# Embedding projection splits behind the last early sum of the norm, and three modulation steps instead of seven in the first output projection

## Chip, cores and metric

The kernel runs on one core of a Trainium2 chip. The metric is the device time of one execution in microseconds, as the median of several runs. Times inside a run are read from a profile of one execution.

## What is computed

Two transformer-like blocks run one after the other on 256 positions of width 1024, in 32-bit floating point. The first block has two layers. Layer 0 is a retention mixer, layer 1 a latent attention (MLA). Each layer ends alike:

```python
x = x + rms_norm(y, post_norm_g[i])
x = x + (p[i] @ ple_w_proj[i]) * jax.nn.sigmoid(x @ ple_w_gate[i])
```

Here `y` is the output projection of the mixer, `p[i] @ ple_w_proj[i]` the embedding projection (from 256 to 1024) and `x @ ple_w_gate[i]` the gate projection (1024 to 1024). The second block begins with a modulation vector that depends on none of this:

```python
mod = jax.nn.silu(c) @ w_ada[l] + b_ada[l]
```

It has 6 × 1024 entries and is needed only when the second block starts. Convolution, pooling, a merge, layer norms and a feed-forward part follow; the change does not touch them.

## The kernel before

Activations are kept transposed: 128 partitions hold 128 features, 256 columns hold the positions. A 32-bit product is made of three products of the rounded type `fp32r` (function `mm`, lines 237 to 239): high part by high part, high weight by low activation, low weight by high activation. So every weight tile of 128 × 1024 (eight blocks of 128 columns) is first split: ScalarE casts it to the high part (line 178, tile `wh`), VectorE subtracts to get the low part (line 179, tile `wl`). Activations are split in the same way (lines 187 and 188). There are five buffers of `wh`, five of `wl` and six of the raw weights (`raw`), which come in by DMAs that SyncE issues. A sixth `wh` can be written only when TensorE has finished with the first.

Each engine works through its own queue in order. A scheduler fixes these queues when the program is built, from the order in which the code calls the operations, from their dependences and from its own estimate of durations.

*Modulation steps.* The modulation vector is made in 48 steps (`ada_steps`), each a DMA of 128 × 1024 weights and one multiply-and-reduce on VectorE (line 418) with two buffers. They are filled in beside other work. `tick` counts the estimated time of the products, and whenever `mods["rate"]` microseconds have gone by since the last step it issues one, up to 41 in the first block. `mod_rate` sets the pace: 7.61 and later 12.84 in the head pairs of MLA, and an own value in each output projection.

*Output projection and norm.* `out_proj` runs the products of the 16 × 8 weight blocks in two parts: for all eight output blocks the first 12 of 16 row blocks, then, after `drain`, the last four. It sets the pace before the first part and takes it away after it. Between the parts `ple_proj` fetches and splits the embeddings. In the second part, each finished pair of output blocks is handed to a `Sums` object: `feed` squares it on ScalarE (line 332) and adds the squares on VectorE (line 336). Pairs 0 to 2 are fed in this way and so there are two additions, the early sums. `flush` has TensorE add them over the partitions by products with a matrix of ones (line 346). Blocks 6 and 7 are squared (line 362) and summed on TensorE directly by `end`, which makes four sum products of 256 columns in all.

*After the projection.* `post` forms 1/rms on VectorE (lines 384, 372, 375, 378; ScalarE's line 386 lies between the first two). While this runs, TensorE has the embedding projection to do: `prepared`, the inner function of `ple_proj`, makes its 48 products of two weight tiles. Then VectorE scales the projection's blocks (line 695), adds the residual (line 696) and splits the result (line 188), and only then can the gate projection (`half_outer`) start, with its own weight tiles. Line 688 of ScalarE copies the projection's blocks out of the accumulators, line 740 those of the embedding projection.

The two places that hand this to the scheduler, in the code before:

```python
            V.tensor_add(self.tot[0], self.tot[0], sq)
...
            tiles = [seq.next() for _ in range(16)]
...
    ys, prep = out_proj("ret_out", ret_g, 12, 1.8, done, 0)
...
    ys, prep = out_proj("mla_out", mla_g, 12, 2.27, done, 1)
```

Of the kernel before, what the change touches and what calls it, by code (L numbers as in the profile page):

```python
# [82 lines left out]
def tile_kernel(ctx, tc, order, xT, pT, pos, vec, cst, cv, rows, wada, wts, outT):  # L83
    nc = tc.nc
    V, A, T = nc.vector, nc.scalar, nc.tensor
# [11 lines left out]
    def nm(s):  # L97
        uid[0] += 1
        return f"{s}_{uid[0]}"
# [4 lines left out]
    def bank2():  # L104
        return bank().rearrange("p (b t) -> p b t", b=2)
# [20 lines left out]
    def two(nb):  # L126
        return Blk(nb, F32R), Blk(nb, F32R)
# [6 lines left out]
    def t2(dt=F32):  # L134
        return tp.tile([P, 2, S], dt, tag="t2", name=nm("t2"), bufs=6)
# [4 lines left out]
    def small(n):  # L140
        return sp.tile([P, n], F32, tag="small", name=nm("sm"), bufs=8)
# [40 lines left out]
    def nouter(name, ms, kbs, c0=0):  # L182
        return [(name, kb * P, c0 + m * P) for m in ms for kb in kbs]

    def split(hi, lo, src, scale=None):
        if scale is None:
            A.copy(hi, src)  # L187
            V.tensor_sub(lo, src, hi.bitcast(F32))  # L188
        else:
            A.activation(hi, src, AF.Copy, scale=scale)  # L190
            V.scalar_tensor_tensor(lo, src, scale, hi.bitcast(F32), MUL, SUB)
# [18 lines left out]
    def mod_rate(us):  # L210
        mods["rate"], mods["last"] = us, clk[0]
# [13 lines left out]
    def drain():  # L225
        busy[0] = True
        while queue:
            due, fn = queue.pop(0)
            clk[0] = max(clk[0], due)
            fn()  # L230
        busy[0] = False
# [4 lines left out]
    def mm(ps, l, r, first, last):  # L236
        T.matmul(ps, l[0], r[0], start=first, stop=False)  # L237
        T.matmul(ps, l[0], r[1], start=False, stop=False)  # L238
        T.matmul(ps, l[1], r[0], start=False, stop=last)  # L239
        tick(3 * cols(r[0]) / 2400.0)  # L240
# [5 lines left out]
    def rhs(pair, kb):  # L246
        return pair[0][kb], pair[1][kb]
# [76 lines left out]
    class Sums:  # L324
# [5 lines left out]
        def feed(self, x):  # L330
            sq = t2()
            A.activation(sq, x, AF.Square)
            if self.tot is None:
                self.tot = [sq, x]
                return
            V.tensor_add(self.tot[0], self.tot[0], sq)
            if self.both:
                new = self.tot[1] if self.own else t2()
                V.tensor_add(new, self.tot[1], x)
                self.tot[1], self.own = new, True  # L340
# [184 lines left out]
    ret_g = two(16)  # L525
# [97 lines left out]
        after(2.04, lambda h=h: ret_av(h))  # L623


    def out_proj(name, pairs, ka, rate, done, layer):
        ys = proj_banks()
        mod_rate(rate)
        seq = Seq(nouter(name, range(8), range(ka)) + nouter(name, range(8), range(ka, 16)))
        for m in range(8):  # L630
            for kb in range(ka):
                mm(ys.at(m), seq.next(), rhs(pairs, kb), ys.starts(m) and kb == 0, False)
        drain()
        mod_rate(None)
        prep = ple_proj(layer)
        for m in range(8):
            for kb in range(ka, 16):
                mm(ys.at(m), seq.next(), rhs(pairs, kb), False, kb == 15 and ys.ends(m))
            if ys.ends(m):
                done(m, ys)  # L640
        return ys, prep
# [20 lines left out]
    def proj_sums(both, get, key):  # L662

        sums = Sums(both, 0)

        def done(m, ys):
            x = get(m, ys)
            if m < 6:
                sums.feed(x)
                if m == 5:  # L670
                    after({"r": 2.0, "m": 0.96}[key], sums.flush)
            elif m == 6:
                after({"r": 1.28, "m": 1.06}[key], lambda: sums.end(x, False))
            else:
                drain()
                sums.end(x, True)
        return sums, done
# [4 lines left out]
    def post(x, ys, sums, layer, prepared):  # L682

        x1 = Blk(DB)

        def scaled(ks):
            for k in ks:
                A.activation(x1[k], ys.at(k), AF.Copy, scale=pgh[:, layer * 8 + k:layer * 8 + k + 1])
        scaled(range(3))
        nry = rms_neg2(sums.ps[0], D)  # L690
        scaled(range(3, DB))
        prj = prepared()
        x1p = two(DB)
        for k, n in ((0, 1), (1, 1), (2, 2), (4, 2), (6, 1), (7, 1)):
            V.tensor_mul(x1.span(k, n), x1.span(k, n), bc2(nry, n))  # L695
            V.tensor_add(x1.span(k, n), x1.span(k, n), x.span(k, n))
            split(x1p[0].span(k, n), x1p[1].span(k, n), x1.span(k, n))
        x2 = Blk(DB)

        def fin(ps, k, n):  # L700
            sgm = t2()[:, :n, :]
            A.activation(sgm, ps, AF.Sigmoid)
            V.tensor_mul(sgm, sgm, prj.span(k, n))
            V.tensor_add(x2.span(k, n), sgm, x1.span(k, n))

        half_outer(f"ple_gate{layer}", x1p, fin)
        return x2
# [14 lines left out]
                    mm(q[:, b, :], seq.next(), rhs(xpair, kb), kb == 0, kb == nk - 1)  # L722
            fin(q, k, n)

    def ple_proj(layer):
        php = [tp.tile([P, 2, S], F32R, tag="fa", name=nm("php"), bufs=3) for _ in range(2)]
        raw = t2()
        nc.gpsimd.dma_start(out=raw, in_=pT[:, 2 * layer:2 * layer + 2, :])
        split(php[0], php[1], raw)

        def prepared():
            seq = Seq(nouter(f"ple_proj{layer}", range(8), range(2)))
            tiles = [seq.next() for _ in range(16)]
            prj = Blk(DB)
            for i in range(4):
                ps = bank2()
                for b in range(2):
                    for kb in range(2):
                        mm(ps[:, b, :], tiles[(2 * i + b) * 2 + kb], (php[0][:, kb, :], php[1][:, kb, :]), kb == 0, kb == 1)
                A.copy(prj.pair(i), ps)  # L740
            return prj
        return prepared

    sums, done = proj_sums(False, lambda m, ys: ys.piece(m), "r")
    ys, prep = out_proj("ret_out", ret_g, 12, 1.8, done, 0)
    xt = post(xt, ys, sums, 0, prep)


# [54 lines left out]
    seq = Seq([e for kb in range(8) for e in (("mla_kr", kb * P, 0), ("mla_in", kb * P, 768), ("mla_in", kb * P, 896))])  # L803
# [9 lines left out]
    seq = Seq(nouter("mla_in", range(6), range(8)))  # L813
# [25 lines left out]
    mla_g = two(16)  # L839
# [116 lines left out]
        after(3.07, lambda p=p: mla_scores(p))  # L956

    sums, done = proj_sums(False, lambda m, ys: ys.piece(m), "m")
    ys, prep = out_proj("mla_out", mla_g, 12, 2.27, done, 1)
    xt = post(xt, ys, sums, 1, prep)  # L960


# [396 lines left out]
    seq = Seq([e for i in range(NA + 2, FB) for e in nouter("w_up", [i, FB + i], range(8))])  # L1359
# [13 lines left out]
    ka = 17  # L1373
    seq = Seq([("w_down", kb * P, 512 * n) for kb in kbs for n in range(2)], 512)
# [30 lines left out]
    for tb in range(2):  # L1405
# [19 lines left out]
        sq, r = small(1), small(1)  # L1425
# [86 lines left out]
```

## Time and profile before

| what | value |
|---|---|
| median of 3 runs | 838.72 us (838.4 to 840.28) |
| time of the profiled execution | 841.12 us |
| its span, first to last instruction | 839.3 us |
| mean granted clock of TensorE | 0.995 |
| TensorE busy, products / weight loads | 824.9 us (98%) / 787.8 us (94%) |
| VectorE busy | 701.7 us (84%) |
| ScalarE busy | 552.0 us (66%) |
| DMA | 167.49 MB, mean 200 GB/s |

Products of TensorE overlap, so its busy time only shows that something was in flight, not that it ran at its best pace. What it lost is seen better where a product starts late after the one before it. In the profile PE is TensorE, DVE is VectorE, ACT is ScalarE, and L336 is line 336 of the kernel. A row of a timeline gives the start and the duration of an instruction (or of several alike, then x3), its tiles as output<-inputs, and in brackets how long the engine had stood idle before it and what ended that.

### The profile page before, as it was taken

The numbers are of one execution on the slowest core, as the hardware profiler recorded it, in microseconds if no ns is written. First come the engines' busy times: TensorE is split into PE (matmuls) and PEld (weight loads), VectorE is DVE, ScalarE is ACT, GpSimd is POOL, SyncE is SP. The second block draws the span as 40 slices with busy tenths as digits, with TensorE's granted clock in tenths as the row PEclk, the third lists the DMA queues.
The fourth block names the chain that finished last, engine by engine and source line by source line (L and its number), as shares of the span: only waits on it lengthen the run. The fifth ranks groups of instructions, "written<-read, shape, count | busy, mean of one in ns | idle before, by whom it ended". The sixth has DMA issues, their size and how long they took to land.

```text
span 839.3 us, 15764 instructions
## 1 busy us (share of the span) xinstructions
PE 824.9 (98%) x6114; PEld 787.8 (94%) x6114; DVE 701.7 (84%) x1283; ACT 552.0 (66%) x967; POOL 9.9 (1%) x30
## 2 busy tenths in 40 slices
PE   8999999999999999999999999999999999999995
PEld 6989899999999999999999999899998999999885
DVE  6999797898889979699864767899687888889986
ACT  7756465645677676788754867998755576666551
POOL 0000000000000000000000000000000000000001
PEclk9999999999999999999999999999999999999999
DMA  8866567778557748365355365245463455567722
GB/s 324 335 241 222 199 245 247 254 257 308 171 187 242 259 150 279 125 226 190 107 195 176 111 216 175 77 166 196 141 242 114 146 184 194 179 221 252 274 81 76
DMA packets 46779, 167.49 MB, mean 200 GB/s; under 512 B 5360, under 2 KB 5616, under 8 KB 46704
## 3 DMA queue, kind: packets, MB, share of 16 engines
q1 hardware_dynamic: 46080, 164.38, 56.1%
q0 software_dynamic: 624, 2.10, 0.8%
q8 instruction: 48, 0.79, 0.4%
q14 instruction: 27, 0.22, 0.1%
HBM read 165.41 MB, written 1.05 MB: 198 GB/s over the span
## 4 chain that ended last, share of the span: by engine, by line
PE 87%; DVE 7%; DMA 3%; ACT 1%; issue 1%; SPq 0%; DVEq 0%
PE ps L238 25%; PE ps L239 24%; PE ps L237 24%; PE ps L243 11%; DMA adach<-in_wada 3%; DVE wl L179 2%; PE ps L346 1%; PE ps L368 1%; DVE adach L418 1%; DMA half<-in_xT 1%; PE ps L925 1%; DVE half L695 0%; ACT wh L178 0%; DVE half L614 0%; DVE t L378 0%
## 5 line engine op out<-in xcount | busy, mean ns | idle before, releaser
L237 PE MATMUL ps<-half,wh 128*128 128x256 f32 x1504 | 424.9, 283 | 0.0
L238 PE MATMUL ps<-half,wh 128*128 128x256 f32 x1504 | 423.4, 282 | 0.6 <-DVE half L188 0.5
L239 PE MATMUL ps<-half,wl 128*128 128x256 f32 x1504 | 421.7, 281 | 0.9 <-DVE wl L179 0.9
L178 ACT CAST wh<-raw 128x1024 fp32r<-128x1024 f32 x233 | 243.2, 1049 | 156.4 <-PE ps L238 91.4
L179 DVE TENSOR_TENSOR wl<-raw,wh 128x1024 fp32r<-128x1024 f32 x233 | 282.3, 1219 | 57.5 <-ACT wh L178 55.3
L238 PEld LDWEIGHTS ps<-half,wh 128*128 128x128 f32 x1504 | 283.2, 188 | 1.9 <-DVE half L188 0.9
L239 PEld LDWEIGHTS ps<-half,wl 128*128 128x128 f32 x1504 | 283.5, 189 | 1.1 <-DVE wl L179 1.1
L237 PEld LDWEIGHTS ps<-half,wh 128*128 128x128 f32 x1504 | 282.7, 188 | 1.2 <-ACT half L187 0.5
L243 PE MATMUL ps<-half,raw 128*128 128x256 f32 (+2 forms) x384 | 84.9, 380 | 0.0
L243 PEld LDWEIGHTS ps<-half,raw 128*128 128x128 f32 x384 | 72.5, 190 | 10.0
L237 PE MATMUL ps<-wh,half 128*128 128x512 f32 (+1 forms) x202 | 73.1, 362 | 1.1 <-ACT wh L178 1.1
L238 PE MATMUL ps<-wl,half 128*128 128x512 f32 (+1 forms) x202 | 71.5, 354 | 0.5 <-DVE wl L179 0.5
L239 PE MATMUL ps<-wh,half 128*128 128x512 f32 (+1 forms) x202 | 71.7, 355 | 0.0
L418 DVE CUSTOM_DVE_ANT_0 adach<-adach,siluc 128x1024 f32<-128x1024 f32 x48 | 58.4, 1218 | 14.2 <-DMA adach<-in_wada 14.2
L237 PEld LDWEIGHTS ps<-wh,half 128*128 128x128 f32 x202 | 38.2, 190 | 7.0 <-ACT wh L178 1.9
L1092 ACT ACTIVATE t<-apad,vec 128x256 f32<-128x256 f32 x106 | 44.2, 498 | 0.5 <-DVE half L1093 0.5
L238 PEld LDWEIGHTS ps<-wl,half 128*128 128x128 f32 x202 | 38.4, 190 | 6.1 <-DVE wl L179 1.0
L239 PEld LDWEIGHTS ps<-wh,half 128*128 128x128 f32 x202 | 38.3, 189 | 5.6
L1093 DVE TENSOR_TENSOR half<-half,t 128x512 f32<-128x512 f32 x53 | 36.4, 687 | 3.7 <-ACT t L1092 1.8
L187 ACT CAST half<-t 128x256 fp32r<-128x256 f32 (+1 forms) x47 | 20.3, 453 | 13.9 <-DVE t L1352 10.9
L188 DVE TENSOR_TENSOR half<-t,half 128x256 fp32r<-128x256 f32 (+1 forms) x47 | 21.6, 481 | 4.0 <-ACT half L187 3.1
L1347 ACT ACTIVATE t<-ps,vec 128x256 f32<-128x256 f32 x38 | 20.9, 556 | 2.0 <-PE ps L239 1.2
(291 smaller groups left out, 905.7 us busy)
## 6 DMA issues: line engine op xcount, KB each, us to landing
raw<-in_wts SPq DMA_DIRECT2D x257, 512.0 KB, 4.2
adach<-in_wada SPq DMA_DIRECT2D x48, 512.0 KB, 5.3
half<-in_xT SPq DMA_DIRECT2D x4, 256.0 KB, 6.0
half<-in_rows POOLq DMA_DIRECT2D x2, 512.0 KB, 4.5
out<-t SPq DMA_DIRECT2D x4, 256.0 KB, 2.0
cst<-in_cst SPq DMA_DIRECT2D x1, 928.0 KB, 11.0
raw<-in_wts SPq DMA_DIRECT2D x2, 256.0 KB, 4.5
siluc<-in_cv SPq DMA_DIRECT2D x1, 512.0 KB, 7.8
```

The source lines that it names most:

```text
L178: A.copy(hi, raw)
L179: V.tensor_sub(lo, raw, hi.bitcast(F32))
L187: A.copy(hi, src)
L188: V.tensor_sub(lo, src, hi.bitcast(F32))
L237: T.matmul(ps, l[0], r[0], start=first, stop=False)
L238: T.matmul(ps, l[0], r[1], start=False, stop=False)
L239: T.matmul(ps, l[1], r[0], start=False, stop=last)
L243: T.matmul(ps, w, r, start=first, stop=last)
L418: V.tensor_tensor_reduce(ch, ch, sc, 1.0, 0.0, MUL, ADD, mod[:, n:n + 1])
L1092: A.activation(t[:, b, :], apad[:, i0 + b, k:k + S], AF.Copy, scale=w[b])
L1093: V.tensor_add(acc.pair(i0 // 2), acc.pair(i0 // 2), t)
L1347: A.activation(t[:, b, :], ps[:, b, :], AF.Identity, bias=col("b_dw_f_2", m), scale=w[2])
```

## The change

It has two parts. First, the 16 calls that take the two weight tiles of the embedding projection out of the sequence now stand in a block that orders their VectorE instructions behind the addition that `feed` made last. So the two splits (line 179) of these tiles come behind the second early sum in VectorE's queue, in both layers. The casts on ScalarE and the DMAs are not ordered by it. `feed` keeps the instruction for this, and `sums` is passed on through `out_proj` and `ple_proj`. Second, the pace of modulation steps in the first output projection goes from 1.8 to 2.27 us, the value that the second one has already. The number of steps up to the end of the first block stays 41.

```diff
--- before.py
+++ after.py
@@ -333,7 +333,7 @@
             if self.tot is None:
                 self.tot = [sq, x]
                 return
-            V.tensor_add(self.tot[0], self.tot[0], sq)
+            self.added = V.tensor_add(self.tot[0], self.tot[0], sq).ins
             if self.both:
                 new = self.tot[1] if self.own else t2()
                 V.tensor_add(new, self.tot[1], x)
@@ -623,7 +623,7 @@
         after(2.04, lambda h=h: ret_av(h))
 
 
-    def out_proj(name, pairs, ka, rate, done, layer):
+    def out_proj(name, pairs, ka, rate, done, layer, sums):
         ys = proj_banks()
         mod_rate(rate)
         seq = Seq(nouter(name, range(8), range(ka)) + nouter(name, range(8), range(ka, 16)))
@@ -632,7 +632,7 @@
                 mm(ys.at(m), seq.next(), rhs(pairs, kb), ys.starts(m) and kb == 0, False)
         drain()
         mod_rate(None)
-        prep = ple_proj(layer)
+        prep = ple_proj(layer, sums)
         for m in range(8):
             for kb in range(ka, 16):
                 mm(ys.at(m), seq.next(), rhs(pairs, kb), False, kb == 15 and ys.ends(m))
@@ -722,7 +722,7 @@
                     mm(q[:, b, :], seq.next(), rhs(xpair, kb), kb == 0, kb == nk - 1)
             fin(q, k, n)
 
-    def ple_proj(layer):
+    def ple_proj(layer, sums):
         php = [tp.tile([P, 2, S], F32R, tag="fa", name=nm("php"), bufs=3) for _ in range(2)]
         raw = t2()
         nc.gpsimd.dma_start(out=raw, in_=pT[:, 2 * layer:2 * layer + 2, :])
@@ -730,7 +730,8 @@
 
         def prepared():
             seq = Seq(nouter(f"ple_proj{layer}", range(8), range(2)))
-            tiles = [seq.next() for _ in range(16)]
+            with tc.issue_after(sums.added):
+                tiles = [seq.next() for _ in range(16)]
             prj = Blk(DB)
             for i in range(4):
                 ps = bank2()
@@ -742,7 +743,7 @@
         return prepared
 
     sums, done = proj_sums(False, lambda m, ys: ys.piece(m), "r")
-    ys, prep = out_proj("ret_out", ret_g, 12, 1.8, done, 0)
+    ys, prep = out_proj("ret_out", ret_g, 12, 2.27, done, 0, sums)
     xt = post(xt, ys, sums, 0, prep)
 
 
@@ -956,7 +957,7 @@
         after(3.07, lambda p=p: mla_scores(p))
 
     sums, done = proj_sums(False, lambda m, ys: ys.piece(m), "m")
-    ys, prep = out_proj("mla_out", mla_g, 12, 2.27, done, 1)
+    ys, prep = out_proj("mla_out", mla_g, 12, 2.27, done, 1, sums)
     xt = post(xt, ys, sums, 1, prep)
```

The scheduler makes new queues from it. In the rows below names ending in numbers are single buffers, and line numbers from 734 on are one higher in the changed kernel.

VectorE, layer 0, from the last output projection weights to 1/rms; before, with the two embedding tiles `wl_2471` and `wl_2477` first, then three gate tiles:

```order
L179 TENSOR_TENSOR wl_2471<-raw_2468,wh_2470 128x1024
L179 TENSOR_TENSOR wl_2477<-raw_2474,wh_2476 128x1024
L179 TENSOR_TENSOR wl_2573<-raw_2570,wh_2572 128x1024
L336 TENSOR_TENSOR t_386_2339<-t_386_2339,t_390_2371 128x512
L179 TENSOR_TENSOR wl_2603<-raw_2600,wh_2602 128x1024
L336 TENSOR_TENSOR t_386_2339<-t_386_2339,t_394_2404 128x512
L179 TENSOR_TENSOR wl_2633<-raw_2630,wh_2632 128x1024
L384 TENSOR_SCALAR t_404_2453<-ps_2434 128x256
L372 TENSOR_TENSOR t_407_2458<-t_405_2455 128x256
L375 TENSOR_TENSOR t_408_2460<-t_404_2453,t_407_2458 128x256
L378 SCALAR_TENSOR_TENSOR t_406_2457<-t_408_2460,t_405_2455 128x256
```

And now, with the embedding tiles `wl_2458` and `wl_2464` behind the two additions, and four gate tiles from `wl_2560` to `wl_2650`:

```order
L336 TENSOR_TENSOR t_382_2326<-t_382_2326,t_386_2358 128x512
L336 TENSOR_TENSOR t_382_2326<-t_382_2326,t_390_2391 128x512
L179 TENSOR_TENSOR wl_2458<-raw_2455,wh_2457 128x1024
L179 TENSOR_TENSOR wl_2464<-raw_2461,wh_2463 128x1024
L179 TENSOR_TENSOR wl_2560<-raw_2557,wh_2559 128x1024
L179 TENSOR_TENSOR wl_2590<-raw_2587,wh_2589 128x1024
L384 TENSOR_SCALAR t_400_2440<-ps_2421 128x256
L179 TENSOR_TENSOR wl_2620<-raw_2617,wh_2619 128x1024
L372 TENSOR_TENSOR t_403_2445<-t_401_2442 128x256
L179 TENSOR_TENSOR wl_2650<-raw_2647,wh_2649 128x1024
L375 TENSOR_TENSOR t_404_2447<-t_400_2440,t_403_2445 128x256
L378 SCALAR_TENSOR_TENSOR t_402_2444<-t_404_2447,t_401_2442 128x256
```

The additions stand together in front. The gate tiles have moved into the chain of 1/rms, and a fourth one, which stood behind the chain, is ahead of line 375. In layer 1 the same happens, one place later: there the gate splits stand ahead of lines 384, 372, 375 and 378, one each, the fourth ahead of line 378.

ScalarE at the same place, before; `wh_2632` is the cast of the third gate tile and `wh_2662` that of the fourth:

```order
L332 ACTIVATE t_394_2404<-ps_1844 128x512
L688 ACTIVATE half_2449<-ps_1844,pgh 128x256
L362 ACTIVATE t_400_2442<-ps_1845 128x256
L688 ACTIVATE half_2449<-ps_1844,pgh 128x256
L688 ACTIVATE half_2449<-ps_1845,pgh 128x256
L178 CAST wh_2632<-raw_2630 128x1024
L322 ACTIVATE sm_2435<-t_386_2339,eps_r 128x1
L362 ACTIVATE t_401_2445<-ps_1846 128x256
L688 ACTIVATE half_2449<-ps_1846,pgh 128x256
L386 ACTIVATE t_405_2455<-ps_2434,eps_r 128x256
L740 COPY half_2480<-ps_2482 128x512
L178 CAST wh_2662<-raw_2660 128x1024
```

And now, with `wh_2619` the third and `wh_2649` the fourth:

```order
L332 ACTIVATE t_390_2391<-ps_1844 128x512
L688 ACTIVATE half_2436<-ps_1844,pgh 128x256
L362 ACTIVATE t_396_2429<-ps_1845 128x256
L688 ACTIVATE half_2436<-ps_1844,pgh 128x256
L322 ACTIVATE sm_2422<-t_382_2326,eps_r 128x1
L688 ACTIVATE half_2436<-ps_1845,pgh 128x256
L178 CAST wh_2619<-raw_2617 128x1024
L362 ACTIVATE t_397_2432<-ps_1846 128x256
L688 ACTIVATE half_2436<-ps_1846,pgh 128x256
L741 COPY half_2467<-ps_2469 128x512
L386 ACTIVATE t_401_2442<-ps_2421,eps_r 128x256
L178 CAST wh_2649<-raw_2647 128x1024
```

The third cast still stands ahead of the square of block 7 (`t_397_2432`), the fourth still behind line 386; line 322 and one copy of line 740 (now 741) have changed places with their neighbours. On TensorE, the two sum products of `flush` have moved three products forward, and the last sum product of layer 0 stands behind eight products of the embedding projection instead of two, that of layer 1 behind two instead of thirteen.

VectorE, layer 0, the first part of the output projection, from the scaling of the last retention head (line 614) on; before:

```order
L614 SCALAR_TENSOR_TENSOR half_1693<-half_1693,t_342_2007 128x512 x2
L418 ISA adach_2132,mod<-adach_2132,siluc 128x1024
L418 ISA mod 128x1
L188 TENSOR_TENSOR half_158<-half_1693,half_154 128x512 x2
L179 TENSOR_TENSOR wl_2203<-raw_2200,wh_2202 128x1024
L418 ISA adach_2159,mod<-adach_2159,siluc 128x1024
L418 ISA mod 128x1
L418 ISA adach_2186,mod<-adach_2186,siluc 128x1024
L418 ISA mod 128x1
L179 TENSOR_TENSOR wl_2240<-raw_2237,wh_2239 128x1024
```

And now:

```order
L614 SCALAR_TENSOR_TENSOR half_1693<-half_1693,t_340_2001 128x512 x2
L179 TENSOR_TENSOR wl_2194<-raw_2191,wh_2193 128x1024
L188 TENSOR_TENSOR half_158<-half_1693,half_154 128x512 x2
L179 TENSOR_TENSOR wl_2227<-raw_2224,wh_2226 128x1024
L179 TENSOR_TENSOR wl_2260<-raw_2257,wh_2259 128x1024
L418 ISA adach_2222,mod<-adach_2222,siluc 128x1024
```

The split of the third weight tile after line 614 (`wl_2240`, now `wl_2227`) has no modulation step between itself and line 614. Up to the embedding splits there are three steps in place of seven. Four have moved to the last head pairs of MLA, among the scaled scores (lines 904 to 914).

## Rows read from the trace of the kernel before

**Rows 1.** Waits of TensorE: engine, tile, line, waited for; total us, times, longest.

```profile
PE ps L239 <- DVE wl L179: 0.9, 1, 0.9
...
PE ps L346 <- DVE t L336: 0.9, 1, 0.9
```

**Rows 2.** Timeline, TensorE, first output projection and norm: start, us, instruction, idle before.

```profile
192.11 0.28 PE L237 MATMUL ps<-half,wh 128*128 128x256 f32 x1
...
192.23 0.28 PE L238 MATMUL ps<-half,wh 128*128 128x256 f32 x1
...
193.43 0.39 PE L239 MATMUL ps<-half,wl 128*128 128x256 f32 x1 [0.92 <-DVE wl L179]
...
211.36 1.53 PE L346 MATMUL ps<-t,ones 128*128 128x256 f32 x6 [0.92 <-DVE t L336]
...
212.54 0.47 PE L237 MATMUL ps<-php,wh 128*128 128x256 f32 x1
...
212.97 0.59 PE L346 MATMUL ps<-t,ones 128*128 128x256 f32 x2
...
219.57 0.39 PE L238 MATMUL ps<-half,wh 128*128 128x256 f32 x1 [0.26 <-DVE half L188]
```

**Rows 3.** Timeline, VectorE, the same stretch.

```profile
191.00 1.23 DVE L418 CUSTOM_DVE_ANT_0 adach<-adach,siluc 128x1024 f32<-128x1024 f32 x1 [1.01 <-DMA adach<-in_wada]
...
205.39 3.49 DVE L179 TENSOR_TENSOR wl<-raw,wh 128x1024 fp32r<-128x1024 f32 x3
...
210.53 0.68 DVE L336 TENSOR_TENSOR t<-t,t 128x512 f32<-128x512 f32 x1
```

**Rows 4.** Timeline, ScalarE, the same stretch.

```profile
208.49 0.59 ACT L332 ACTIVATE t<-ps 128x512 f32<-128x512 f32 x1
...
210.37 1.05 ACT L178 CAST wh<-raw 128x1024 fp32r<-128x1024 f32 x1
...
216.15 1.05 ACT L178 CAST wh<-raw 128x1024 fp32r<-128x1024 f32 x1 [0.78 <-PE ps L238]
```

**Rows 5.** Timeline, TensorE, second norm.

```profile
470.44 0.59 PE L346 MATMUL ps<-t,ones 128*128 128x256 f32 x2
...
475.84 0.39 PE L238 MATMUL ps<-half,wh 128*128 128x256 f32 x1 [0.28 <-DVE half L188]
```

**Rows 6.** Timeline, VectorE, second norm.

```profile
472.50 0.42 DVE L375 TENSOR_TENSOR t<-t,t 128x256 f32<-128x256 f32 x1
...
472.96 0.43 DVE L378 SCALAR_TENSOR_TENSOR t<-t,t 128x256 f32<-128x256 f32 x1
...
475.37 0.75 DVE L188 TENSOR_TENSOR half<-half,half 128x256 fp32r<-128x256 f32 x2
```

**Rows 7.** Timeline, ScalarE, second norm.

```profile
465.44 0.59 ACT L332 ACTIVATE t<-ps 128x512 f32<-128x512 f32 x1
...
472.29 1.05 ACT L178 CAST wh<-raw 128x1024 fp32r<-128x1024 f32 x1 [0.29 <-PE ps L238]
...
476.20 0.58 ACT L740 COPY half<-ps 128x512 f32<-128x512 f32 x1
```

**Rows 8.** Timeline, VectorE, scores of a late head pair.

```profile
400.44 0.17 DVE L909 RECIPROCAL sm<-sm 128x2 f32<-128x2 f32 x1 [0.46 <-ACT sm L907]
...
403.34 0.17 DVE L909 RECIPROCAL sm<-sm 128x2 f32<-128x2 f32 x1 [0.73 <-ACT sm L907]
...
403.54 0.55 DVE L914 TENSOR_SCALAR sm<-sm,sm 128x128 f32<-128x128 f32 x2
```

**Rows 9.** Timeline, TensorE, transposes of the same head pair.

```profile
405.62 0.82 PE L925 MATMUL ps<-ident,sm 128*128 128x128 f32 x6
```

**Rows 10.** Windows: us, busy by engine (instructions), granted clock, DMA share, GB/s.

```profile
5.00:11.00 6.00, 4.38 (x12) 1.73 (x10) 3.54 (x8) 4.29 (x9) 0.00 (x0) 1.00 0.99 352
...
11.00:15.80 4.80, 4.27 (x13) 3.14 (x12) 4.80 (x12) 4.14 (x7) 0.00 (x0) 0.66 1.01 392
...
208.00:220.00 12.00, 10.83 (x82) 10.23 (x81) 10.20 (x19) 9.02 (x19) 0.00 (x0) 1.00 0.61 219
```

## Prediction

> **What bounds the kernel now.** TensorE sets the time. I read the waits of TensorE first, then its timeline, then the timelines of the two engines that feed it. Its products of 256 columns start 0.12 us apart, as the first two show [rows 2], and the waits list has only two entries near 1 us inside the program that this change can touch [rows 1]. Both lie in the first output projection and the norm behind it. At 192.23 a product waits for a split that VectorE could not begin, because a modulation step ahead of it in VectorE's queue waited 1.01 us for its data [rows 2, 3]; TensorE loses 193.43 − 192.23 − 0.12 = 1.08. At 211.36 the first sum product waits 0.92 for the last addition of squares (line 336), which stands behind three splits back to back and one more [rows 2, 3]. In front of the gate projection come the small waits at 219.57 and 475.84 [rows 2, 5]. So perhaps 2.5 us could be won, and the question is what the new queue orders cost.
>
> **The change, part by part.** Times below are on the clock of the profile shown, whose own run took 841.12 us; that is 2.4 above the median of 838.72, so I sum differences and add them to the median. About 1.7 us, 0.2%, is what a measurement of this kernel can tell from no change.
>
> *Pace 2.27 instead of 1.8.* The order shows three modulation steps in VectorE's queue between the last retention head and the embedding splits where there were seven. At 192 the steps ahead of the needed split are gone: it stands right behind the splits of the head, and its cast is long made. That wait goes: **−1.08**. If another stall took its place, this term would be 0. The four steps reappear behind the scores of the last head pairs. There VectorE scales the probabilities until 403.54 + 0.55 = 404.09, and the transposes begin at 405.62: 1.53 in hand, and 0.27 more for the second three [rows 8, 9]. Three steps at 1.14 each (a pitch taken from VectorE's splits of the same size: 3.49 for three, less overlap [rows 3]) are 3.42; VectorE's idle time there takes up 0.46 + 0.73 [rows 8]. That leaves 0.43 late; the splits that move around it could make it nothing. I take **+0.3**, ends 0 and 1.3 (a data wait like the 1.01 at 191.00 on top [rows 3]).
>
> *The splits behind the last early sum, first norm.* The addition now follows the one before it at once. Its square ends on ScalarE at 208.49 + 0.59 = 209.08 [rows 4]; 0.68 for the addition and 0.15 to TensorE (211.36 against 210.53 + 0.68 [rows 2, 3]) give 209.94, and TensorE gets there at about that time: the 0.92 wait is gone. But the new order of TensorE puts three weight products between the sum products, and eight embedding products instead of two ahead of the last one. A sum product takes 0.39 (three in 212.54 − 211.36), and two embedding products with the change of operand type 0.43 [rows 2], so 0.19 for the change. 209.94 + 2 × 0.39 + (0.19 + 3 × 0.12) + 0.39 + (0.19 + 8 × 0.12) = 212.81. The last sum is at **212.8, where it was at 212.97**: little of the gain is left, and ScalarE could not serve it much sooner, since a cast of 1.05 now stands ahead of its last square [rows 4].
>
> Then comes the step that decides. Behind the sum VectorE forms 1/rms in four operations (lines 384, 372, 375, 378), scales, adds the residual and splits; only then can the gate products run. Before, all three gate splits that have a buffer stood ahead of this chain, and the fourth behind it. Now a *fourth* gate split stands ahead of line 375. It needs a cast (line 178), and the cast a weight buffer: there are five, the two embedding tiles and three gate tiles hold them, so the fourth must wait until TensorE has finished the first embedding tile, 24 of the 48 embedding products. The trace shows this wait: the cast at 216.15 was released by TensorE, 3.18 after the last sum product [rows 2, 4]. With six more embedding products ahead of the sum it comes 3.18 − 6 × 0.12 = 2.46 after it: 215.27. Cast 1.05, split 1.14: line 375 starts at 217.46. From there the order is the one that the second norm already has in this trace: 475.37 − 472.50 = 2.87 to the first split, 0.47 more to the product behind it [rows 5, 6]. So 220.80 instead of 219.57: **+1.23**. TensorE's own work would be done at 212.81 + 0.39 + 0.19 + 40 × 0.12 = 218.2, so it stands still for over 2 us.
>
> *Second norm.* The addition moves from behind a split to 465.44 + 0.59 = 466.03 [rows 7]; with 0.68 and 0.15 TensorE can start summing at 466.86. Five products lie between, one sum product, two embedding products: 466.86 + 0.78 + 0.79 + 0.39 + 0.43 = 469.25 for the last sum (470.44 before [rows 5]). Here the fourth split stands even later in the chain, ahead of line 378. Its cast came 472.29 − 470.44 = 1.85 after the last sum, with thirteen embedding products ahead of that; now two, so 1.85 + 11 × 0.12 = 3.17 after it: 472.42 [rows 5, 7]. Plus 1.05 and 1.14: line 378 at 474.61. From it 475.37 − 472.96 = 2.41, and 0.47 [rows 5, 6]: 477.49. ScalarE also has a fifth cast and a copy of 0.58 [rows 7] ahead of the cast of the first block, both waiting for the end of the embedding products, which could add some 0.3. 477.6 against 475.84: **+1.8**.
>
> The bounds: the delay is nothing (each norm as before, less the early sum) or as computed plus a split's 1.14 in each, if the queue waits once more. No arithmetic, no transfer and no semaphore of its own is added; the splits are only ordered on VectorE.
>
> Sum: −1.08 + 0.3 + 1.23 + 1.8 = **+2.3**, and 838.72 + 2.3 = **841.0 us**.
>
> **TensorE's clock.** Rows first: in the stretch before 11 us TensorE was busy 4.38 of 6.00, and in the next 4.80 the granted clock averaged 0.66, a part of it at 1.2 GHz; around the stalls of the first norm, 10.83 busy of 12.00, it stayed at 1.00, 2.4 GHz [rows 10]. The Trainium skill (TensorE: Matmul & The Clock Gate, Part 1) says that idle TensorE falls back to half rate and advises against long gaps between bursts. By it the stalls made here would also slow what follows; the trace agrees at the start of the program, and no row of before shows a stall of over 2 us later on. The sum above goes without it, since the only longer stalls shown left the clock alone; as a rival it is priced below.
>
> **Rivals.**
> 1. *The embedding products cover the chain* (not slower). If the fourth split turned out not to hold lines 375 and 378, each chain would run from the last sum as it does now: 219.57 − 212.97 = 6.60 and 475.84 − 470.44 = 5.40 [rows 2, 5]. The first norm would give 219.41 (−0.16), the second 474.65, bounded by TensorE's own end (469.25 + 0.39 + 0.19 + 46 × 0.12 = 475.35, about −0.3). With −1.08 and +0.3 this is −1.2, 837.5 us; without the term for the last heads, and with the last square served a split's time earlier, −2.3, 836.4. It decides at the point where the fourth cast ends before line 384 has finished. Against it stands the release by TensorE at 216.15 [rows 4]; for it, only that an inferred releaser could be wrong. Chance 0.12.
> 2. *The chain is held, but for less*: the buffer is free sooner, or line 375 is reached later anyway. Half of 1.23 + 1.8 gives +0.7, 839.5. Chance 0.2.
> 3. *The forecast*, 841.0, itself 840.4 to 842.2. Chance 0.45.
> 4. *The clock falls as well.* The mean 0.66 over 4.80 us means about 3.3 us at half rate [rows 10], so 1.6 lost for each fall. One fall gives 842.6, two 844.2. For it: the stalls grow to twice what the trace has shown harmless. Against: weight products run densely on both sides. Chance 0.18.
> 5. *The slower pace does not help*: the reduced steps still wait for data, in another place ahead of a needed split, and the 1.08 stays: 842.1. The first norm's gain is then gone too. The step's own data wait of 1.01 [rows 3] speaks for it, four fewer transfers in that stretch against it. Chance 0.05.
>
> **How the numbers follow.** Slower by more than 1.7 (above 840.4) are case 3, less its lower edge, and cases 4 and 5: 0.63. Within 1.7 (837.0 to 840.4) are case 2, the lower edge of 3 and most of case 1: 0.30. Faster is the far end of case 1: 0.07. The range leaves out that far end and the second clock fall: 838.6 to 843.6.
>
> **What would show it.** Right: TensorE's waits at 192 and 211 gone; two new waits of 1.5 to 2.5 us in front of the gate products, released by line 188 on VectorE or line 187 on ScalarE; on VectorE a split ahead of line 375 (first norm) and line 378 (second) whose idle time is ended by a cast, and that cast released by TensorE. Wrong: if lines 375 and 378 follow line 372 without an idle stretch, the decisive step has failed; if the last sum lands more than 0.5 before 212.8 plus the shift of the stretch, the cost of the first norm is too high; if the granted clock leaves 1.00 behind a norm, case 4 is at work.

## The result and the profile after

The changed kernel takes **845.07 us** (844.0 to 846.06), the kernel before in the same comparison 839.55 (838.4 to 840.5): a ratio of 1.0054, 95% interval 1.0034 to 1.0074, so some 2.9 to 6.2 us more. The forecast was 841.0 in a range of 838.6 to 843.6: right in its direction, too small in its size. The profiled execution has a span of 843.2 against 839.3, of which 0.55 in the other direction comes from the start of the program, where TensorE ran at half rate for a while in the profile before (granted clock 0.66 from 11 to 15.8 us [rows 10]) and not in this one (1.00).

The waits of TensorE after (total us, times, longest):

```profile
PE ps L237 <- ACT half L187: 3.8, 2, 1.9
...
PE ps L239 <- DVE wl L179: 0.8, 1, 0.8
```

The waits of [rows 1] are gone (what is left for line 179 lies at 30 us). In their place stand two of 1.9, one in each norm, in front of the gate products. TensorE's timeline, first norm:

```profile
211.00 0.70 PE L346 MATMUL ps<-t,ones 128*128 128x256 f32 x2
...
216.13 0.28 PE L239 MATMUL ps<-php,wl 128*128 128x256 f32 x1
218.33 0.63 PE L237 MATMUL ps<-half,wh 128*128 128x256 f32 x3 [1.92 <-ACT half L187]
...
221.40 0.41 PE L237 MATMUL ps<-half,wh 128*128 128x256 f32 x1
221.62 0.41 PE L238 MATMUL ps<-half,wh 128*128 128x256 f32 x1
...
222.25 0.28 PE L238 MATMUL ps<-half,wh 128*128 128x256 f32 x1
222.37 0.28 PE L239 MATMUL ps<-half,wl 128*128 128x256 f32 x1
```

The last embedding product starts at 216.13, the first gate product at 218.33. Then something that [rows 2] do not have: gate products start 0.21 apart until 222.04 and 0.12 apart again from 222.25. The windows over the two norms give the clock (columns as in [rows 10]):

```profile
217.00:221.00 4.00, 2.52 (x12) 2.31 (x13) 4.00 (x11) 2.23 (x5) 0.00 (x0) 0.73 0.76 307
221.00:225.00 4.00, 4.00 (x31) 4.00 (x31) 3.06 (x6) 1.73 (x3) 0.00 (x0) 0.85 0.04 5
474.00:478.00 4.00, 2.15 (x18) 1.94 (x16) 3.97 (x9) 3.09 (x6) 0.00 (x0) 1.00 0.97 362
478.00:482.00 4.00, 4.00 (x22) 3.95 (x22) 4.00 (x9) 0.62 (x1) 0.00 (x0) 0.57 0.33 133
```

Behind both waits the granted clock leaves 1.00: for a time TensorE runs at 1.2 GHz, 22 products in 478 to 482 where 36 have room. What made the wait is on VectorE, first norm:

```profile
207.35 0.69 DVE L336 TENSOR_TENSOR t<-t,t 128x512 f32<-128x512 f32 x1 [2.13 <-ACT t L332]
207.96 4.62 DVE L179 TENSOR_TENSOR wl<-raw,wh 128x1024 fp32r<-128x1024 f32 x4
212.51 0.42 DVE L384 TENSOR_SCALAR t<-ps 128x256 f32<-128x256 f32 x1
212.84 1.21 DVE L179 TENSOR_TENSOR wl<-raw,wh 128x1024 fp32r<-128x1024 f32 x1
213.97 0.41 DVE L372 TENSOR_TENSOR t<-t 128x256 f32<-128x256 f32 x1
214.63 1.23 DVE L179 TENSOR_TENSOR wl<-raw,wh 128x1024 fp32r<-128x1024 f32 x1 [0.24 <-ACT wh L178]
215.77 0.42 DVE L375 TENSOR_TENSOR t<-t,t 128x256 f32<-128x256 f32 x1
```

Between the last addition and line 375 stand six splits, 1.14 each, with 0.24 of idle time in all. ScalarE beside it:

```profile
212.96 0.48 ACT L386 ACTIVATE t<-ps,eps_r 128x256 f32<-128x256 f32 x1 [0.16 <-DVE t L384]
213.55 1.05 ACT L178 CAST wh<-raw 128x1024 fp32r<-128x1024 f32 x1
...
216.38 1.04 ACT L178 CAST wh<-raw 128x1024 fp32r<-128x1024 f32 x1 [0.75 <-PE ps L238]
217.33 0.58 ACT L741 COPY half<-ps 128x512 f32<-128x512 f32 x1
217.87 0.74 ACT L187 CAST half<-half 128x256 fp32r<-128x256 f32 x2
```

The cast of the fourth gate split (213.55) follows line 386 with no wait for TensorE. The last product that reads the buffer which this cast needs is in the trace too, and so is the same place in the second norm (VectorE, then ScalarE):

```profile
213.19 0.28 PE L238 MATMUL ps<-php,wh 128*128 128x256 f32 x1
...
473.57 0.42 DVE L375 TENSOR_TENSOR t<-t,t 128x256 f32<-128x256 f32 x1
473.97 1.22 DVE L179 TENSOR_TENSOR wl<-raw,wh 128x1024 fp32r<-128x1024 f32 x1
475.11 0.42 DVE L378 SCALAR_TENSOR_TENSOR t<-t,t 128x256 f32<-128x256 f32 x1
...
476.24 0.75 DVE L696 TENSOR_TENSOR half<-half,half 128x256 f32<-128x256 f32 x2
...
472.88 1.06 ACT L178 CAST wh<-raw 128x1024 fp32r<-128x1024 f32 x1 [0.75 <-PE ps L238]
...
476.65 0.58 ACT L741 COPY half<-ps 128x512 f32<-128x512 f32 x1
477.13 0.71 ACT L187 CAST half<-half 128x256 fp32r<-128x256 f32 x2
```

In the second norm VectorE has no idle time between line 375, the fourth gate split and line 378, though the cast of that split was released by TensorE. And the new x, whose first block VectorE has added by 476.66 (the first of the two at 476.24), is cast only at 477.13, right behind a copy. In the first norm the cast follows within 0.09 us (217.78, 217.87), so ScalarE adds some 0.4 of its own in the second.

### The profile page after: what moved, and what is told of

It reads as the page before. It is cut to its first block, busy times and chain, and to the rows that moved or that the text cites. A ratio compares the mean times of both kernels' runs of the same rounds, so it can differ in the third digit from the quotient of the medians.

```text
span 843.2 us, 15759 instructions
## 1 busy us (share of the span) xinstructions
PE 827.5 (98%) x6114; PEld 790.3 (94%) x6114; DVE 700.6 (83%) x1283; ACT 553.1 (66%) x967; POOL 9.9 (1%) x30
## 4 chain that ended last, share of the span: by engine, by line
PE 89%; DVE 5%; ACT 2%; DMA 2%; issue 1%; SPq 0%; DVEq 0%; ACTq 0%
PE ps L238 25%; PE ps L239 25%; PE ps L237 25%; PE ps L243 11%; DVE wl L179 1%; DMA raw<-in_wts 1%; PE ps L346 1%; PE ps L368 1%; ACT wh L178 1%; DMA half<-in_xT 1%; DMA adach<-in_wada 1%; PE ps L926 1%; DVE adach L418 0%; DVE half L695 0%; PE ps L1176 0%
```

## The experiments

Each ran beside the kernel before on one chip; ratios are to that. The table comes from the traces: how much later than in the trace before a product of the same number in TensorE's order starts, at the end of a stretch less at its beginning (us; stretches on the clock before, added products left out). "Clock" is TensorE's granted clock, the mean over all runs. Each row is one profiled execution: from 235 to 420 us the kernels lose at three places, near 285, 325 and 386 us, which change from profile to profile, so that a difference of some tenths in that column says little.

| kernel | ratio, interval | 185–206 | first norm 206–235 | 235–420 | second norm 462–495 | clock |
|---|---|---|---|---|---|---|
| before | 1 | 0 | 0 | 0 | 0 | 0.997 |
| changed | 1.0054, 1.0034–1.0074 | −1.21 | 2.53 | −0.21 | 2.97 | 0.993 |
| changed, again (e9) | 1.0045, 1.0028–1.0063 | −1.21 | 2.69 | −0.27 | 3.03 | 0.994 |
| e1 pace alone | 0.9975, 0.9958–0.9993 | −1.21 | −0.80 | 0.85 | 0.00 | 0.997 |
| e2 order alone | 1.0037, 1.0015–1.0060 | −0.58 | 1.40 | 0.26 | 3.04 | 0.994 |
| e6 order in first norm | 1.0013, 0.9999–1.0027 | −1.21 | 2.43 | 0.08 | 0.01 | 0.996 |
| e7 order in second norm | 1.0012, 0.9999–1.0026 | −1.21 | −0.79 | 0.73 | 1.51 | 0.995 |
| e4 gate splits behind 1/rms | 1.0011, 0.9992–1.0031 | −1.21 | 2.81 | 0.53 | 0.04 | 0.995 |
| e8 and ScalarE's order | 0.9995, 0.9984–1.0005 | −1.21 | 0.19 | 0.60 | 0.05 | 0.997 |
| e3 waits filled, 8 long | 1.0052, 1.0034–1.0070 | −1.21 | 1.99 | 1.89 | 2.75 | 0.996 |
| e5 waits filled, 4 long | 1.0052, 1.0033–1.0071 | −1.21 | 1.19 | 1.12 | 1.51 | 0.996 |
| e10 waits filled, 14 short | 1.0035, 1.0024–1.0047 | −1.21 | 1.13 | 0.70 | 1.51 | 0.997 |
| e11 pace alone and 14 short | 1.0013, 0.9998–1.0028 | −1.21 | 0.26 | 1.24 | 0.93 | 0.997 |

**e1: the pace alone.**

```diff
-            with tc.issue_after(sums.added):
-                tiles = [seq.next() for _ in range(16)]
+            tiles = [seq.next() for _ in range(16)]
```

> The pace of 2.27 alone, with the splits queued as before. Theory A (the two parts are independent; the slower pace removes the stall of 1.08 at 192 us, the harm sits in the two norms): the stall at 192 is gone, both norms look as before with the 0.92 wait at 211 and no wait over 0.6 in front of the gate products, the four moved steps cost 0 to 0.3, and the time is 838.3 to 838.8 against 839.55 for the kernel before. Theory B (part of the loss is the moved steps in the last head pairs): TensorE stands still for 1 us or more between 390 and 415 us, and the time is 840 or more.

Measured: ratio 0.9975, some 2.1 us gained, where 0.75 to 1.25 were expected; the interval, 0.6 to 3.5 us, holds both. The wait at 192 is gone. The one at 211, which was expected to stay, shrinks from 0.92 to 0.15 us, though the embedding splits still stand ahead of the addition. VectorE, first norm, in this kernel:

```profile
204.63 0.68 DVE L336 TENSOR_TENSOR t<-t,t 128x512 f32<-128x512 f32 x1
206.31 1.23 DVE L179 TENSOR_TENSOR wl<-raw,wh 128x1024 fp32r<-128x1024 f32 x1 [1.00 <-ACT wh L178]
207.45 0.68 DVE L336 TENSOR_TENSOR t<-t,t 128x512 f32<-128x512 f32 x1
...
210.53 0.42 DVE L384 TENSOR_SCALAR t<-ps 128x256 f32<-128x256 f32 x1 [0.17 <-PE ps L346]
```

In [rows 3] three splits ran back to back into the addition: VectorE was behind. The trace before has six modulation steps of 1.14 each between 188 us and the addition, that of e1 three. Both wait for the data of such steps (1.01 and 1.68 before, 2.95 in e1), so it is the number of steps that differs. With three fewer VectorE is early, idles 1.00 before a split and makes the addition at 207.45. Of the two stalls that bounded the kernel the pace removes one and all but 0.15 of the other; hardly anything is left for the second part of the change to win. Most of the 0.85 in the next stretch is a wait of 0.56 at 285 us for a split of the latents, which stands behind a weight split there; between 390 and 415 us TensorE doesn't stand still for the moved steps.

**e2: the order alone.**

```diff
-    ys, prep = out_proj("ret_out", ret_g, 12, 2.27, done, 0, sums)
+    ys, prep = out_proj("ret_out", ret_g, 12, 1.8, done, 0, sums)
```

> The splits behind the last early sum alone, with the pace of 1.8. Theory A: both norms show the wait of about 2 us in front of the gate products and about 18 products at half rate behind each; the stall at 192 is back. Time of the changed kernel plus 1.1: 845.7 to 846.7. Theory B (the moved steps carry a part): 844 or less. If the steps that now stand near the norm delay its splits, the waits in front of the gate products would be longer than 2.0.

Measured: 1.0037, 845.26 us where its baseline was 841.13. By this difference of 4.1 the time is under what theory A gave (6.1 to 7.1 over 839.55) and within theory B; by the trace theory A holds, since both waits are there, but half of the stall at 192 stays away (−0.58). Nor do the two parts add up: 0.9975 and 1.0037 give 1.0012 together, 3.5 us under the changed kernel. In the traces 1.4 of these are counted twice (the stall at 211, 0.80 in e1's first norm, and the 0.58 at 192, which each part removes by itself); the rest is not explained and lies within the intervals. TensorE in the first norm:

```profile
216.65 0.28 PE L239 MATMUL ps<-php,wl 128*128 128x256 f32 x1
218.85 0.62 PE L237 MATMUL ps<-half,wh 128*128 128x256 f32 x3 [1.92 <-ACT half L187]
219.63 0.39 PE L238 MATMUL ps<-half,wh 128*128 128x256 f32 x1 [0.16 <-DVE half L188]
219.85 0.28 PE L239 MATMUL ps<-half,wl 128*128 128x256 f32 x1
219.97 0.28 PE L237 MATMUL ps<-half,wh 128*128 128x256 f32 x1
```

The same wait of 1.92, but products 0.12 apart right behind it: here the clock stayed at 2.4 GHz, and the first norm costs 1.40, not 2.53. In the second norm of the same execution it fell (0.57 in 478 to 482), and that costs 3.04.

**e6, e7: the order in one norm only** (with the pace of 2.27; e7 has `layer == 1`).

```diff
-            with tc.issue_after(sums.added):
+            if layer == 0:
+                with tc.issue_after(sums.added):
+                    tiles = [seq.next() for _ in range(16)]
+            else:
                 tiles = [seq.next() for _ in range(16)]
```

> Pace 2.27, and the splits behind the last early sum in the first norm only. By the traces of the changed kernel and of the pace alone the first norm costs 3.6 us (wait 2.0 and half-rate products 1.7), the second nothing: pace alone (ratio 0.9975, -2.1 us) + 3.6 = +1.5 us, ratio 1.0018, where the first wait lets the clock fall; +0.1 us, ratio 1.000, where it does not. Rival: the two norms are not independent (the first one's delay shifts the transfers of what follows), and the sum of both single costs misses the changed kernel by over 1.5 us.

> Pace 2.27, and the splits behind the last early sum in the second norm only. By the traces the second norm costs 3.0 us (wait 2.0, half-rate products 1.7, less the small wait of 0.4 that is there anyway and 0.3 of the sum): -2.1 + 3.0 = +0.9 us, ratio 1.001. Rival: as for the first norm; a ratio under 0.999 or over 1.0035 would show that the norms hang together.

Measured: 1.0013 and 1.0012. Each norm adds 0.0038 or 0.0037 to the pace alone; 0.9975 + 0.0038 + 0.0037 = 1.0050, between the two measurements of the changed kernel. That shows no sign of the norms hanging together. In e6's profile the clock fell behind the wait, in e7's it did not, and its norm costs 1.51.

**e4: the gate splits behind 1/rms** (`formed` is line 378's instruction).

```diff
...
+                if formed is not None and seq.i >= 8:
+                    with tc.issue_after(formed):
+                        w = seq.next()
...
```

> The changed kernel with the splits of the gate tiles, from the second tile on, queued behind the last operation of 1/rms (line 378 of the changed kernel); the embedding splits and the first gate split stay behind the last early sum. Theory E (1/rms is late because VectorE works through splits back to back between the last addition and it, 1.14 us each): with three of the six gone, the chain ends about 2.1 us earlier, the wait in front of the gate products is 0 to 0.9 in each norm, too short for the clock to fall, and the time is 845.07 - 2 x 1.7 (clock) - 2 x (1.1 to 2.0) = 837.7 to 839.5. Theory F (the first gate products wait for ScalarE, whose copies and casts follow the end of the embedding products): the waits stay at 1.5 us or more and the time above 843.

Measured: 1.0011. The second norm is as before (0.04), as theory E says. But there ScalarE's queue changed with the edit: x's cast (475.57) now stands ahead of the last copy (476.22), so the run took both delays away and does not tell them apart. The first keeps its wait of 1.85, though 1/rms ends at 213.87 instead of 216.65 (0.7 of that is an earlier start). ScalarE there (line 749 is the copy of line 741 in the changed kernel):

```profile
215.69 1.04 ACT L178 CAST wh<-raw 128x1024 fp32r<-128x1024 f32 x1 [0.75 <-PE ps L238]
216.65 0.58 ACT L749 COPY half<-ps 128x512 f32<-128x512 f32 x1
217.12 0.71 ACT L187 CAST half<-half 128x256 fp32r<-128x256 f32 x2
```

The cast of the new x stands behind a weight cast that waits for TensorE to release a buffer, and behind the copy of the last embedding block: theory F, in this norm.

**e8: ScalarE's order too.** The same, and (`second` is the cast of x's second block, the last lines stand for the later gate tiles):

```diff
+                second = split_last[0]
+                with tc.issue_after(second):
+                    A.copy(prj.pair(3), lastps)
...
+                        with tc.issue_after(second):
+                            w = seq.next()
```

> The run with the gate splits behind 1/rms, and on ScalarE the copy of the last embedding block and the casts of the later gate tiles queued behind the first two casts of the new x (line 187 of the changed kernel). Theory G (in the first norm the chain is early there, but the cast of x stands in ScalarE's queue behind a cast and a copy that wait for the end of the embedding products): the first norm's wait falls from 1.9 to 0.3 to 1.0, no half-rate products follow, and the time is 1.0 to 2.7 us under the run with the gate splits alone, a ratio of 0.998 to 1.000 to the kernel before. Theory H (something else holds the first gate product): the wait stays at 1.9 and the ratio at 1.001 or above.

Measured: 0.9995. TensorE in the first norm (lines 239, 241 and 189 are 237, 239 and 187 of the changed kernel):

```profile
216.41 0.28 PE L241 MATMUL ps<-php,wl 128*128 128x256 f32 x1
217.51 0.50 PE L239 MATMUL ps<-half,wh 128*128 128x256 f32 x2 [0.83 <-ACT half L189]
```

The wait is 0.83, the clock stays up, the norm costs 0.19: theory G. So in the changed kernel two queues hold the first gate products, VectorE by the splits and ScalarE right behind it: in the first norm ScalarE holds alone when VectorE is early (e4), in the second its cast comes 0.47 after VectorE has added x. ScalarE's order put right alone was not run; by the timeline VectorE would still add x only after the last embedding product has started (216.13 and 475.46), at 217.78 and 476.66. With both put right the kernel stands where it was before; the order still wins nothing over the pace alone.

**e3, e5: the wait filled with products of constants** (e5 has four).

```diff
+        for _ in range(8):
+            T.matmul(sums.ps[0], ones, cos4, start=True, stop=True)
```

> The changed kernel with eight products of constants (0.216 us each, 1.7 us, into the bank of the norm's sum that was read before) ahead of the first gate product in both layers, so that TensorE is busy through most of the wait; the wait itself is not touched. Theory C (the clock falls because TensorE stands still for 2 us, and the half-rate products behind it are its cost): the gate products still begin at the same time, but all at the full pitch of 0.12, the granted clock stays at 1.00, and each norm gives back 18 x 0.095 = 1.7 us: 845.07 - 3.4 = 841.7. Theory D (the products behind the wait are slow for another cause, such as freshly written operands): the pitch of 0.21 stays for some 18 products behind the wait, and the time is 845 or more.

> As the run with eight products of constants, but with four: eight took 3.3 us of TensorE where the wait is 2.0, so that they held the gate products up themselves. Four take 1.7. Theory C (standing still for 2 us makes the clock fall): the gate products begin where they do in the changed kernel, no product behind runs at the pitch of 0.21, and the time is 2.5 to 3.5 us under that of the changed kernel, a ratio of 1.0015 to 1.003 to the kernel before. Theory D (the fall has another cause): half-rate products as in the changed kernel, ratio 1.005.

Measured: 1.0052 (1.0034 to 1.0070) and 1.0052 (1.0033 to 1.0071). e3 was mis-sized: each such product is two of 0.216 in the trace, and they hold the gate products up. In both, no half-rate products follow the norms and the mean clock is 0.996: theory C as to the clock. But e5 is no faster than the changed kernel: as to the time neither theory C nor D has the number. In its trace the norms are 2.8 us shorter than in the changed kernel, and 1.3 of that is lost again from 235 to 420 us, most of it at the place shown for e10 below.

**e9, e10, e11: the same question on one chip.** e9 is the changed kernel; e10 has

```diff
+        for _ in range(14):
+            T.matmul(sums.ps[0], php[0][:, 0, :P], php[1][:, 0, :], start=True, stop=True)
```

and e11 the same lines in e1's kernel, where there is no wait to fill.

> The changed kernel itself, on the same chip as the next two. Ratio to the kernel before 1.0034 to 1.0074 as measured before. Theory C (a wait of 2 us is near the point where the clock falls, and it falls in most of them): the mean clock over the runs is about 0.993 to 0.994, where the kernel before shows 0.9965 to 0.997.

> The changed kernel with fourteen products of 0.118 us (1.65 in all) in each wait, of the same form as the weight products. Theory C: the mean clock over the runs is back at 0.996 to 0.997, no half-rate products follow the norms, and the time is 2 to 3 us under the changed kernel of this call. Theory I (the half-rate products cost nothing in the end, because the 1.4 us that each norm saves without them is lost again in later waits for data): the clock is back, the two norms are shorter in the trace, and the time is within 1 us of the changed kernel.

> The same fourteen products in the kernel with the pace alone, where there is no wait for them to fill: a control for what they cost by themselves. They lie on TensorE's path, 2 x (1.65 + 0.2), less the small waits of 0.4 that they cover: ratio 0.9975 + 0.0030 to 0.0045 = 1.0005 to 1.002. A ratio over 1.003 would show that the products cost more than their time, and that the runs with filled waits understate what the clock gives back.

Measured: 1.0045, 1.0035 and 1.0013 (0.9998 to 1.0028), the clock 0.994, 0.997 and 0.997. e10 in the first norm:

```profile
216.55 1.80 PE L694 MATMUL ps<-php,php 128*128 128x256 f32 x14
218.63 0.61 PE L237 MATMUL ps<-half,wh 128*128 128x256 f32 x3 [0.27 <-ACT half L187]
219.41 0.38 PE L238 MATMUL ps<-half,wh 128*128 128x256 f32 x1 [0.17 <-DVE half L188]
219.63 0.28 PE L239 MATMUL ps<-half,wl 128*128 128x256 f32 x1
```

The gate products begin no sooner than without the filling, but at full pitch: 1.13 and 1.51 in the two norms, 1.56 and 1.52 less than in e9. That is the price of one fall of the clock, shown by taking the idle time away and leaving the delay. The medians are only 1.1 apart (843.85 against 844.97), and the intervals overlap. But the 3.1 us belong to a profiled execution of e9 with two falls, and its average execution has fewer. One fall takes 0.43 × 4 = 1.7 us of full clock (the window 478 to 482 above), 0.002 of the mean; the mean clocks over the runs, 0.9938 in e9 and 0.9966 in e10, are 0.0028 apart. That makes 1.4 falls or 2.1 us, an estimate. One place where a part of it is lost is in the trace. VectorE in e10, a modulation step of a late head pair:

```profile
383.11 1.23 DVE L418 CUSTOM_DVE_ANT_0 adach<-adach,siluc 128x1024 f32<-128x1024 f32 x1 [0.95 <-DMA adach<-in_wada]
```

and the same step in e9:

```profile
383.14 1.23 DVE L418 CUSTOM_DVE_ANT_0 adach<-adach,siluc 128x1024 f32<-128x1024 f32 x1
```

The program is there a microsecond sooner and waits for the same data; TensorE pays 0.96 of it at 385.85. What is left of the estimate, 1.1, is what the medians show, but the intervals are too wide to decide between theory C and theory I as to the time. The control e11 lies where the products' own time puts it, so the filling shows no hidden cost. How much of a saved fall reaches the end, between 0 and 3 us, stays open.

## Why the prediction was too small

- *The stall at 192* (−1.08): gone, −1.21 in the trace. Right.
- *The moved modulation steps* (+0.3): TensorE doesn't wait for them between 390 and 415 us (e1). The term should have been 0, its lower end; the cover seen in [rows 8, 9] was enough.
- *The first norm* (+1.23 without the clock): e10 measures 1.13 with the clock held up. The first gate products were put at 220.80, less the 1.08 and the 0.55 that the start differs 219.17; the timeline has that product at 219.11. Its cause was only half right. The forecast let the fourth split's cast wait for TensorE and left out of the sum the time that VectorE needs for six splits. In the trace that cast follows line 386, thus the splits ahead of line 384, and the buffer came free at 213.19 + 0.28 = 213.47, within 0.1 us of the cast at 213.55. In the second norm TensorE does release the cast (472.88), but the cast ends just when VectorE, which has had no break, comes to the split (473.97). The prediction had named lines 375 and 378 without idle time ahead of them as a sign against its decisive step; the second norm shows it, the first has 0.24. So the buffer and the splits' own time end together in both norms. That the number came out so well is in this respect luck, and no run separates the two. That the wait goes when VectorE's and ScalarE's queues are both put right is shown by e4 in the second norm and by e8 in the first.
- *The second norm* (+1.8): 1.51 where the clock stayed (e7, e10). Line 378 was put at 474.61, with the 0.55 by which this stretch begins later 475.16; it starts at 475.11. Behind it come the 0.4 that ScalarE adds, for which the forecast had put 0.1 into the sum.
- *TensorE's clock*: here is **the step that failed**. "The sum above goes without it, since the only longer stalls shown left the clock alone": those were of 1.08, and the stalls forecast were of over 2 us. Behind nine such waits of 2.0 in the profiles (two each in the changed kernel, e9 and e2, one each in e4, e6 and e7) the clock fell seven times; behind e8's, where the product starts are 1.10 apart and not 2.13 to 2.20 as in the nine, it didn't. With the waits filled (e3, e5, e10: six norms) it never fell. One fall costs 1.5, near the 1.6 taken from [rows 10]. Without the falls the four stretches give −1.21 + 1.13 + 1.51 − 0.21 = 1.2, less than the sum of 2.3. With them: −1.21 + 2.53 + 2.97 − 0.21 = 4.1, and some 0.4 from a place near 600 us that most kernels here share with it. Rival 4 with two falls, 844.2, was the nearest case (the mean clocks, 0.9933 of the changed kernel and 0.9967 of the kernel before in 85 runs, make 1.7 falls an execution, an estimate at 0.002 each); it had a chance of 0.18 for one fall and two together, and the range left the second fall out. The rule of the Trainium skill cited there (TensorE: Matmul & The Clock Gate, Part 1), that an idle TensorE falls back to half rate, told in the right direction; the trace agrees (0.57 from 478 to 482 us). The advice of the Trainium skill in the same part is against longer gaps than these; here waits of 2.0 were enough in seven of nine cases.
- *The first rival* (the embedding products cover the chain) was wrong for the changed kernel, and is what e8 comes near to.
- *Slips in the sums*, none of which moves the forecast: 209.08 + 0.68 + 0.15 is 209.91, not 209.94, and in the first rival 475.35 is 0.49 before 475.84, not 0.3.

The baseline adds to the miss: the kernel before was 838.72 in the runs shown and 839.55 in this comparison.

## What to carry over

Before work is queued behind a sum, count what then stands between that sum and the next thing the bottleneck needs, in every queue: six splits of 1.14 (6.8) are longer than the 48 embedding products of 0.12 (5.8) that were to cover them. When two edits aim at neighbouring stalls, ask whether the first already removes the cause of the second: here three modulation steps fewer let VectorE catch up, and the pace alone is the best version measured, 0.9975 of the kernel before. And when a forecast makes a stall longer than any that the trace shows, the row that says "the clock stayed" no longer speaks for it; its price belongs into the sum.

## What the runs showed of the hardware

Behind waits of TensorE of the same length, 2.0 us after dense work, the clock fell in some executions and not in others: in e2 not in the first norm and yes in the second. The six runs of the changed kernel have mean clocks of 0.992 to 0.996, those of the kernel before 0.996 to 0.998 in 75 of 85. A stall of this length has two prices, 1.5 and 3.0 us in the second norm, and its mean is seen only over many runs. In e4 the fall came late: the first dozen products behind the wait ran at full pitch, then came some 16 at 0.21.
